# One load per branch, written ahead in the order of use, and the embedding's work beside the last expert, in the mixture-of-experts layer of a two-layer decoder on one Trainium2 core

## The chip, the cores and the metric

The kernel runs on one core of one Trainium2 chip. Its engines are TensorE (PE for the products, PEld for the loads of the stationary operand), VectorE (DVE), ScalarE (ACT), GpSimd (POOL) and SyncE (SP, which issues most transfers). The metric is device microseconds of one execution, lower is better. Three runs of the kernel before took 1607.78 to 1609.05 us, with a median of 1608.46 us.

## The reference, cut to what matters

Two layers over 256 tokens of 1024 channels. Layer 0 has a dense SwiGLU, layer 1 a mixture of 8 experts of which each token takes 2. After the feed-forward part both layers add an embedding that is gated by the residual stream.

```python
def swiglu(x, w1, w3, w2):
    return (jax.nn.silu(x @ w1) * (x @ w3)) @ w2

def moe_swiglu(x, router, w1, w3, w2):
    logits = (x @ router).astype(jnp.float32)
    top_vals, top_idx = lax.top_k(logits, TOP_K)
    ...
    for e in range(N_EXPERTS):
        y = y + comb[..., e:e + 1] * swiglu(x, w1[e], w3[e], w2[e])
...
        x = layer_norm(ALPHA * x + f.astype(x.dtype), ln_g[i, 1], ln_b[i, 1])
        e = (p[i] @ ple_proj[i]) * jax.nn.sigmoid(x @ ple_gate_w[i] + ple_gate_b[i])
        x = layer_norm(ALPHA * x + e.astype(x.dtype), ln_g[i, 2], ln_b[i, 2])
```

Everything is f32. w1 and w3 of an expert are 1024 x 3584, w2 is 3584 x 1024, so one expert reads 42 MB of weights and eight read 336 MB.

## The kernel before, in words

The profile's first 600 us are layer 0 and the mixer of layer 1, which the change does not touch. Then comes `moe`. The router finds each expert's tokens, `gather` (L1393) collects an expert's up to 128 tokens with one-hot products, for two experts at a time (`pair`), and `expert` multiplies them.

**Weights.** An expert has 42 loads of [128, 2048] f32, 1 MB each (`expert_loads`): for each of three chunks of 1024 hidden columns 4 loads of w1 and 4 of w3, for the last chunk of 512 columns 2 and 2, then 14 loads of w2. They are issued by SP at L249 (`load`) into a ring of 18 tiles (`self.ring`): two `rb`, four `st`, `pp`, `ra`, four `hl`, `xl`, two `re`, two `over` and one `raw` of the layer's own pool. A load can start when the products on its tile's previous load are done. The first 8 loads (`EARLY`) are written ahead of the router, every other one just before its use. The order in which each engine's queue holds its instructions is made by the framework's scheduler from its own estimate, so the order of writing is not always the order of issue.

**Branches.** TensorE alone branches on the expert's number of tokens (`either`, L1412): with up to 64 tokens two products run side by side on half the array each ("few"), with more they run one after the other ("many"). One branch holds two loads (`GRP = 2`), that is 21 branches per expert. Work that is to stand between branches (transposes of the hidden tile, the scatter of an expert's result) lies in a list `todo`, which `flush` empties after a branch.

**PSUM.** Six banks go round: a pair for w1, one for w3, one for w2, two for the scatter. `gate` work (Silu on ACT, product on DVE, L1475 and L1476) stands right behind a chunk's products. A pair's unused halves are cleared first (L1432).

**Expert 6.** At `e == OVF` the list is emptied, a branch over the overflow code (more than 128 tokens for one expert) is taken on all engines (L1538, L1539), and the two `over` tiles are free for loads only behind it. Expert 6's first 16 loads are written ahead of it.

**End.** Behind the last expert come its scatter and the second layer norm (`norm`, L524 to L532, `make_xT` L334), `ple_late` (the embedding's input and projection are loaded, split into a high and a low part, L313 and L314, and multiplied, `pp`), then `ple_gate`: the gate's weights are split (`square_parts`, high part L551 on ACT, low part `glo` L553 on POOL and DVE), multiplied for the first and then the second 128 tokens (`pg`, L308 to L310 and L565), and the last layer norm writes the output.

Of the kernel before, what the change touches and what calls it, by code (L numbers as in the profile page):

```python
# [7 lines left out]
F32 = mybir.dt.float32  # L8
F32R = mybir.dt.float32r
# [145 lines left out]
EARLY = 8  # L155
# [3 lines left out]
GRP = 2  # L159
# [21 lines left out]
CHUNKS = ((0, 1024), (1024, 1024), (2048, 1024), (3072, 512))  # L181

# [10 lines left out]
class Trunk:  # L193
# [58 lines left out]
    def room(self, dt, name):  # L252

        pool, tag, n = self.ring[self.nload % len(self.ring)]
        self.nload += 1
        return pool.tile([P, 2048], dt, tag=tag, name=name, bufs=n)

# [846 lines left out]
    def ple_late(self, l):  # L1104

        a = self.a
        n = 2 * S
        self.ring, self.nload = self.turned((self.xp, "pp")), 0
        self.pp = self.xp.tile([P, TT, D], F32, tag="pp", name="pp")
        pT = list(self.parts(self.load(a["pT"][l].rearrange("(k p) t -> p k t", p=P), 2, S), 2, S, self.nc.gpsimd))  # L1110
        w = list(self.parts(self.load(a["ple_proj"][l].rearrange("(k p) f -> p k f", p=P), 2, D), 2, D, self.nc.gpsimd))
        yield
        for tt in range(TT):
            ts = slice(tt * P, (tt + 1) * P)
            for h in range(2):
# [4 lines left out]
                self.nc.scalar.activation(self.pp[:, tt, hs], ps, AF.Copy, scale=0.5)  # L1120
                yield
# [17 lines left out]
    def ple_gate(self, l, raws, low, normed, bias, lnp):  # L1139
# [3 lines left out]
        sp = self.square_parts(range(KT), lambda k: raws[k // 2][:, k % 2], low)  # L1143
        for k in range(KT):

            with self.after(*normed) if k >= GK[l] else ExitStack():
                parts = next(sp)
# [88 lines left out]
    def moe(self, l, mp):  # L1236
# [7 lines left out]
        self.ring.append((mp, "raw", 1))  # L1244
        self.pre = [self.load(*s) for s in self.expert_loads(j, 0)[:EARLY]]
# [92 lines left out]
        for e in range(NE):  # L1338
            if e == OVF:

                self.flush()
                ov = self.over
                main = self.turned(ov[:2])
                self.ring, self.nload = main, 0
                self.pre = [self.load(*s) for s in self.expert_loads(j, e)[: len(main)]]
                self.ring, self.nload = [ov] * ov[2], 0
                pre, self.pre = self.pre, []
                self.overflow(j, mp, Da[:, e // 2 % 2], cint, th, tl, rank, sel, comb, y)
                self.ring, self.pre, self.nload = main + self.ring, pre, len(main)
# [11 lines left out]
            self.expert(mp, self.expert_loads(j, e), n, self.xh[:, :, es], De, [D2[:, tt] for tt in range(TT)], ce, y, ahead, norm if last else None)  # L1361
            if e == NE - 2:

                lnp = self.ln_params(l, 1, mp, "tl")
                more = mp.tile([P, 2, D], F32R, tag="th", name="more")
# [325 lines left out]
```

## Time and profile before

| | us |
|---|---|
| median of 3 runs | 1608.46 |
| the profiled execution | 1610.99 |
| its span from the first to the last instruction | 1608.8 |
| PE busy in the span | 1454.2 (90%) |
| DVE / ACT / POOL busy | 678.0 / 401.3 / 266.0 |
| moved by transfers | 445.28 MB, mean 277 GB/s |

A row of a view of stretches has the stretch in us from the span's start, its length, then for PE, PEld, DVE, ACT and POOL the busy time with the number of instructions, the granted TensorE clock as a share of 2.4 GHz, the busy share of the 16 DMA engines, and GB/s. A row of the timeline has start, duration, engine, line, operation, what it writes and reads, and in brackets the idle time before it and what ended it. A row of the groups has count, busy time, mean ns of one, and the idle time before with what ended it. Ends of products are modelled, so a product's row can overlap the next one's.

### The profile page before, as it was taken

Reading aid. Unit: us, or ns where it says so; the run is one execution under the profiler, and the core shown is the slowest. Engines: PE = TensorE matmul, PEld = TensorE weight load, DVE = VectorE, ACT = ScalarE, POOL = GpSimd, SP = SyncE. Lnnn points to the kernel's source line nnn. Section 1 sums busy time; section 2 is a strip of 40 time slices with the busy share of each in tenths; the row PEclk is TensorE's granted clock in tenths of the full one; section 3 lists DMA queues with packets and bytes.
Section 4 is the critical chain, followed back from the end, with each engine's and each line's share of the span. In section 5 each row is a group of like instructions: output and inputs, shape, how many; then the busy total and the mean of one; then the engine's idle time right before and its main releaser. Section 6 shows DMA issues by size and latency. Waiting matters only on the chain. (4 is left out here: it accounts for less than half of the span.)

```text
span 1608.8 us, 16526 instructions
## 1 busy us (share of the span) xinstructions
PE 1454.2 (90%) x6318; PEld 832.5 (52%) x6319; DVE 678.0 (42%) x1105; ACT 401.3 (25%) x719; POOL 266.0 (17%) x205
## 2 busy tenths in 40 slices
PE   6776999999888699998899999999999998998776
PEld 6544788876675475432344643444644454342234
DVE  8989648646778955222121103121102102122137
ACT  6454555434466431100001001000000000000023
POOL 4855106612124511000000000000000000010012
PEclk9787999999998888999999999999999999999999
DMA  7431365553462049999999999999898878999971
GB/s 250 137 152 40 124 214 187 192 170 131 170 192 111 27 158 401 403 408 405 407 409 402 409 344 389 408 410 400 299 308 272 301 238 281 362 408 409 402 288 53
DMA packets 139625, 445.28 MB, mean 277 GB/s; under 512 B 7408, under 2 KB 19312, under 8 KB 138496
## 3 DMA queue, kind: packets, MB, share of 16 engines
q1 hardware_dynamic: 138496, 437.42, 73.3%
q0 software_dynamic: 1024, 6.38, 1.1%
q8 instruction: 76, 1.25, 0.3%
q14 instruction: 29, 0.24, 0.0%
HBM read 442.72 MB, written 1.05 MB: 276 GB/s over the span
## 5 line engine op out<-in xcount | busy, mean ns | idle before, releaser
L1468 PE MATMUL mgu<-wraw,xe 128*64 128x512 f32 (+3 forms) x2048 | 548.5, 542 | 25.4 <-DMA wraw<-in_moe_w_dram 17.3
L1468 PEld LDWEIGHTS mgu<-wraw,xe 128*64 128x64 f32 (+1 forms) x2048 | 238.3, 157 | 318.4 <-issue 246.9
L1503 PE MATMUL mo<-wraw,ht 128*64 128x512 f32 (+1 forms) x896 | 272.0, 595 | 12.4 <-DMA wraw<-in_moe_w_dram 12.4
L1503 PEld LDWEIGHTS mo<-wraw,ht 128*64 128x64 f32 (+1 forms) x896 | 101.0, 157 | 172.0 <-issue 143.1
L314 DVE TENSOR_TENSOR whl<-wraw,whl 128x1024 fp32r<-128x1024 f32 (+2 forms) x106 | 136.5, 1297 | 81.7 <-ACT whl L313 81.1
L313 ACT ACTIVATE whl<-wraw 128x1024 fp32r<-128x1024 f32 (+3 forms) x109 | 107.5, 994 | 138.3 <-PE fffn_w L310 44.6
L1476 DVE TENSOR_TENSOR hb<-hb,mgu 128x512 f32<-128x512 f32 (+1 forms) x64 | 37.9, 618 | 236.1 <-PE mgu L1468 235.7
L510 POOL DMA_DIRECT2D lnp<-in_lnp_dram x5 | 2.8, 566 | 772.6 <-ACT xe L1397 744.1
L1449 ACT ACTIVATE ht<-hT 128x512 f32<-128x512 f32 (+1 forms) x32 | 17.4, 544 | 393.4 <-PE hT L1444 378.0
L314 DVE TENSOR_TENSOR ot<-mo,ot 128x512 fp32r<-128x512 f32 x16 | 10.6, 688 | 243.1 <-ACT ot L313 243.1
L1432 DVE MEMSET mgu<- 64x512 f32 x128 | 62.1, 485 | 100.2 <-ACT hb L1475 84.1
L1447 DVE COPY ht<-hT 128x512 f32<-128x512 f32 (+1 forms) x32 | 20.0, 625 | 140.7 <-PE hT L1444 136.7
L310 PE MATMUL fffn_w<-whl,xh 128*128 128x512 f32 (+1 forms) x192 | 71.8, 374 | 0.0
L309 PE MATMUL fffn_w<-whl,xl 128*128 128x512 f32 (+1 forms) x192 | 71.7, 373 | 0.0
L308 PE MATMUL fffn_w<-whl,xh 128*128 128x512 f32 (+1 forms) x192 | 71.4, 372 | 0.0
L1475 ACT ACTIVATE hb<-mgu 128x512 f32<-128x512 f32 (+1 forms) x64 | 32.4, 543 | 152.1 <-PE mgu L1468 149.0
L313 ACT ACTIVATE ot<-mo 128x512 fp32r<-128x512 f32 x16 | 9.0, 596 | 239.6 <-PE mo L1503 239.6
L957 DVE SCALAR_TENSOR_TENSOR cy<-upad,pk,cy 128x256 f32<-128x256 f32 x60 | 56.6, 943 | 1.2
L308 PEld LDWEIGHTS fffn_w<-whl,xh 128*128 128x128 f32 x192 | 36.1, 188 | 6.7
L309 PEld LDWEIGHTS fffn_w<-whl,xl 128*128 128x128 f32 x192 | 36.1, 188 | 6.6
L310 PEld LDWEIGHTS fffn_w<-whl,xh 128*128 128x128 f32 x192 | 36.1, 188 | 6.2
L1444 PEld LDWEIGHTS hT<-sqr,hb 128*128 128x128 f32 x224 | 24.8, 140 | 24.7 <-issue 20.4
(371 smaller groups left out, 2147.0 us busy)
## 6 DMA issues: line engine op xcount, KB each, us to landing
wraw<-in_moe_w_dram SPq DMA_DIRECT2D x336, 1024.0 KB, 17.5
wraw<-in_ffn_w_dram SPq DMA_DIRECT2D x33, 1024.0 KB, 5.2
wraw<-in_cmp_w_dram SPq DMA_DIRECT2D x8, 1024.0 KB, 5.6
wraw<-in_w_out_dram SPq DMA_DIRECT2D x8, 1024.0 KB, 7.2
wraw<-in_ple_gate_w_dram SPq DMA_DIRECT2D x8, 1024.0 KB, 5.0
wraw<-in_w_in_dram SPq DMA_DIRECT2D x8, 792.0 KB, 5.9
wraw<-in_w_in_dram SPq DMA_DIRECT2D x8, 768.0 KB, 8.0
lnp<-in_lnp_dram POOLq DMA_DIRECT2D x5, 1024.0 KB, 5.2
```

The source lines that it names most:

```text
L308: mm(dst, xh, wh, start=start, stop=False)
L309: mm(dst, xl, wh, start=False, stop=False)
L310: return mm(dst, xh, wl, start=False, stop=stop)
L313: h = self.hi = self.nc.scalar.activation(dh, src, AF.Copy)
L314: return h, (low or self.nc.vector).tensor_tensor(dl, src, dh.bitcast(F32), op=ALU.subtract)
L957: nc.vector.scalar_tensor_tensor(y0, u(0, k), w(0, k), y0, op0=ALU.mult, op1=ALU.add)
L1432: nc.vector.memset(acc[h][rows[1 - h]], 0.0)
L1444: nc.tensor.transpose(ps[:, i * P : (i + 1) * P], hbs[h][:, i * P : (i + 1) * P], self.ident)
L1468: mm(dst, x, wk, start=k == 0, stop=k == KT - 1)
L1475: nc.scalar.activation(hb[:, :hw], accs[0][h][:, :hw], AF.Silu)
L1476: nc.vector.tensor_mul(hb[:, :hw], hb[:, :hw], accs[1][h][:, :hw])
L1503: mm(dst, x, w[:, i, h * 512 : (h + 1) * 512], start=k == 0, stop=k == NK - 1)
```

## The change

1. The ring gives way to a list of loads (`specs`) and a list of free tiles (`slots`). `feed` writes loads into free tiles, `take` hands the next one to its branch, `give` returns its tile behind the branch and feeds again. So 18 loads are written ahead of the router, and each later one right behind the branch that frees its tile.
2. One load per branch: 42 branches per expert, two loads' work no longer share one.
3. `flush` runs only what was in the list; what these items append waits for the next branch. The gate work, the transposes, the copies out of PSUM, the split of an expert's result, its scatter and its additions each move one branch later than the one ahead. The round of PSUM banks moves on by two after the scatter.
4. The embedding's input, projection and gate weights (0.25 + 1 + 4 MB) stand in the list ahead of the last expert's 14 loads of w2. `ple_early` writes their split and the embedding's products between that expert's last branches, the low parts going into tiles that come free at the end. For the last expert the tiles `pp`, `hl` and `xl` are no longer refilled, so 12 are left, and 8 once the gate's four raw tiles are held.

```diff
@@ -152,11 +152,10 @@
-EARLY = 8
...
-GRP = 2
+LOADS = 42
...
+DOWN = D_FFE // P // 2
@@ -254,6 +255,31 @@
+    def feed(self):
...
+        while self.slots and self.nspec < len(self.specs):
+            pool, tag, n = slot = self.slots.pop(0)
+            if slot == self.over and OVF * LOADS <= self.nspec and self.kept is not None:
+                self.kept.append(slot)
+            elif tag not in ("pp", "hl", "xl") or self.nspec < (NE - 1) * LOADS:
+                src, a, b = self.specs[self.nspec]
+                v = pool.tile([P, 2048], F32, tag=tag, name="wraw", bufs=n)[:, : a * b].rearrange("p (a b) -> p a b", a=a)
+                self.nc.sync.dma_start(v, src)
+                self.fifo.append((v, slot))
+                self.nspec += 1
...
+    def give(self):
+        self.slots += self.used
+        self.used = []
+        self.feed()
@@ -1101,15 +1127,23 @@
-    def ple_late(self, l):
...
+    def ple_early(self, l, mp):
...
+        pT, w = [list(self.parts(self.take(), 2, b)) for b in (S, D)]
+        self.give()
+        raws = [self.take() for _ in range(4)]
+        self.used = []
+        yield
         self.pp = self.xp.tile([P, TT, D], F32, tag="pp", name="pp")
...
+        sp = self.square_parts(range(KT), lambda k: raws[k // 2][:, k % 2], low)
+        for k in range(KT):
+            while k % 2 == 0 and not self.slots:
+                yield
+            self.gate_parts = next(sp)
+            if k % 2:
                 yield
@@ -1241,8 +1291,12 @@
-        self.ring.append((mp, "raw", 1))
-        self.pre = [self.load(*s) for s in self.expert_loads(j, 0)[:EARLY]]
+        self.specs = [s for e in range(NE) for s in self.expert_loads(j, e)]
+        self.specs[-DOWN:-DOWN] = self.ple_specs(l)
+        self.nspec, self.fifo, self.kept, self.used = 0, [], [], []
+        self.slots = self.turned() + [(mp, "raw", 1)] + [(self.st, "hl", HB)] * HB + [(self.cp, "xl", 1)]
+        self.feed()
@@ -1401,8 +1449,10 @@
     def flush(self):
-        while self.todo:
-            self.todo.pop(0)()
+        todo, self.todo = self.todo, []
+        for f in todo:
+            f()
@@ -1455,82 +1520,100 @@
-                for u0 in range(0, KT // ku, GRP):
-                    ws = get()
+                for u in range(KT // ku):
+                    w = get()
...
+            self.todo.append(lambda ci=ci, hw=hw, accs=accs: gate(ci, hw, accs))
         acc = pair("mo")
         NK = D_FFE // P
-        for g in range(0, NK // 2, GRP):
-            ws = get()
+        for g in range(NK // 2):
+            if late:
+                next(late, None)
+            w = get()
...
+        def result():
+            for h in range(2):
+                ot = mp.tile([P, 2, 512], F32R, tag=f"h{h}", name="ot", bufs=1)
+                self.split(ot[:, 0], ot[:, 1], acc[h])
+                ots.append(ot)
+            self.todo.append(scatter)
...
+            def adds():
+                for tt in range(TT):
+                    for h in range(2):
+                        add(tt, h, scs[tt][h])
...
+                self.turn += 2
```

## Rows read from the trace of the kernel before

**Rows 1.** The page: GB/s in 40 equal slices of the span, 40.2 us each

```profile
GB/s 250 137 152 40 124 214 187 192 170 131 170 192 111 27 158 401 403 408 405 407 409 402 409 344 389 408 410 400 299 308 272 301 238 281 362 408 409 402 288 53
```

**Rows 2.** Stretches of experts 1, 2 and 5, and of expert 7 in two parts

```profile
709.00:809.00 100.00, 82.71 (x407) 30.33 (x404) 17.49 (x36) 8.48 (x17) 0.00 (x0) 1.00 1.03 407
809.00:960.00 151.00, 150.58 (x410) 74.54 (x412) 21.19 (x39) 8.19 (x16) 0.00 (x0) 1.00 1.01 394
...
1199.00:1350.00 151.00, 149.94 (x408) 74.06 (x406) 19.73 (x36) 7.88 (x15) 0.00 (x0) 1.00 0.84 277
...
1441.00:1512.00 71.00, 59.69 (x296) 22.66 (x292) 17.62 (x31) 7.28 (x14) 3.44 (x2) 1.00 1.03 405
1512.00:1548.00 36.00, 27.95 (x118) 7.36 (x116) 1.18 (x3) 1.01 (x2) 0.52 (x1) 1.00 1.03 408
```

**Rows 3.** The same view behind the start of expert 6

```profile
1366.00:1370.00 4.00, 4.00 (x22) 1.29 (x18) 0.00 (x0) 0.00 (x0) 0.00 (x0) 1.00 0.91 323
1370.00:1376.00 6.00, 6.00 (x30) 2.01 (x28) 0.00 (x0) 0.00 (x0) 0.00 (x0) 1.00 0.69 272
1376.00:1380.00 4.00, 4.00 (x20) 1.29 (x18) 0.00 (x0) 1.08 (x2) 0.00 (x0) 1.00 0.80 269
```

**Rows 4.** Waits of SP's queue from 1349 to 1385: total, times, longest us

```profile
SPq L249 <- PE mgu L1468: 16.3, 4, 8.2
```

**Rows 5.** Waits of PE from 809 to 1350, and its branches in that stretch (min/median/max)

```profile
PE mgu L1468 <- DVE mgu L1432: 2.1, 2, 1.5
PE DT L1486 <- ACT ht L1449: 1.0, 4, 0.3
PE mgu L1468 <- ACT hb L1475: 0.7, 1, 0.7
...
L1412 PEldq COMPARE_BRANCH  x146: 65/169/340, 811.5 to 1341.7; - x146
```

**Rows 6.** Transfers issued from 1529 to 1560: count, KB each, us to landing

```profile
wraw<-in_ple_gate_w_dram SPq DMA_DIRECT2D x4, 1024.0 KB, 16.6
...
wraw<-in_ple_proj_dram SPq DMA_DIRECT2D x1, 1024.0 KB, 17.2
wraw<-in_pT_dram SPq DMA_DIRECT2D x1, 256.0 KB, 16.9
```

**Rows 7.** Timeline behind the last expert: its last product, then the layer norm

```profile
1546.09 1.94 PE L1503 MATMUL mo<-wraw,ht 128*64 128x512 f32 x8 [0.66 <-DMA wraw<-in_moe_w_dram]
...
1552.88 0.21 DVE L524 BATCH_NORM_AGGREGATE mv<-bst 128x2 f32<-128x12 f32 x1
1553.12 2.79 DVE L531 SCALAR_TENSOR_TENSOR x<-x,mv,lnp 128x512 f32<-128x512 f32 x1
...
1559.38 0.75 DVE L532 SCALAR_TENSOR_TENSOR x<-x,rs,lnp 128x512 f32<-128x512 f32 x1
```

**Rows 8.** Groups from 1546 to 1609: POOL's low parts, ACT's tables, PE's embedding products

```profile
L553 POOL TENSOR_TENSOR glo<-wraw,whi 128x512 fp32r<-128x512 f32 x8 | 11.8, 1512 | 8.9 <-ACT whi L551 8.9
...
L310 PE MATMUL pp<-whl 128*128 128x512 f32 x8 | 4.4, 554 | 3.5 <-POOL whl L314 3.5
...
L526 ACT ACT_TABLE_LOAD x3 | 3.8, 1283 | 0.1
```

**Rows 9.** Timeline of the gate's products: start, 13 without a wait, second half

```profile
1566.19 0.73 PE L565 MATMUL pg<-more,sqr 33*128 33x512 f32 x2
...
1584.12 0.39 PE L308 MATMUL pg<-whi,xh 128*128 128x512 f32 x1
...
1586.91 0.39 PE L310 MATMUL pg<-glo,xh 128*128 128x512 f32 x1
1587.23 0.50 PE L565 MATMUL pg<-more,sqr 33*128 33x512 f32 x1
```

**Rows 10.** Stretches behind the last expert, 4 us each

```profile
1556.00:1560.00 4.00, 2.20 (x6) 1.49 (x5) 3.94 (x3) 0.60 (x1) 2.13 (x1) 0.61 0.17 32
1560.00:1564.00 4.00, 4.00 (x13) 3.20 (x12) 0.13 (x1) 0.89 (x2) 0.00 (x0) 0.54 0.57 232
```

More of the change, by code (lines that the diff above doesn't have):

```diff
@@ L1137, in ple_bias, with ple_gate @@
         return out
-    def ple_gate(self, l, raws, low, normed, bias, lnp):
+    def ple_gate(self, l, raws, low, normed, bias, lnp, parts=None):
         nc = self.nc
         x = self.x
-        sp = self.square_parts(range(KT), lambda k: raws[k // 2][:, k % 2], low)
+        sp = iter(()) if parts else self.square_parts(range(KT), lambda k: raws[k // 2][:, k % 2], low)
         for k in range(KT):
-            with self.after(*normed) if k >= GK[l] else ExitStack():
-                parts = next(sp)
+            with self.after(*normed) if k >= GK[l] and not parts else ExitStack():
+                parts = next(sp, parts)
         for tt in range(TT):
@@ L1339, in moe @@
             if e == OVF:
[L1341 to L1347, printed above, removed]
+                while self.todo:
+                    self.flush()
+                self.ring, self.nload = self.kept, 0
                 self.overflow(j, mp, Da[:, e // 2 % 2], cint, th, tl, rank, sel, comb, y)
-                self.ring, self.pre, self.nload = main + self.ring, pre, len(main)
+                self.slots, self.kept = self.slots + self.kept, None
+                self.feed()
                 pair(e)
@@ L1360, in moe @@
             last = e == NE - 1
-            self.expert(mp, self.expert_loads(j, e), n, self.xh[:, :, es], De, [D2[:, tt] for tt in range(TT)], ce, y, ahead, norm if last else None)
+            late = self.ple_early(l, mp) if last else None
+            self.expert(mp, None, n, self.xh[:, :, es], De, [D2[:, tt] for tt in range(TT)], ce, y, ahead, norm if last else None, late)
             if e == NE - 2:
                 lnp = self.ln_params(l, 1, mp, "tl")
-                more = mp.tile([P, 2, D], F32R, tag="th", name="more")
-                bias = self.ple_bias(l, mp.tile([P, D], F32, tag="h2", name="gb"), more[:, 0])
-        advance(self.ple_late(l))
-        raws = list(self.ple_load(l))
-        low = [t[:, i] for t in [self.room(F32R, "glo").rearrange("p (a d) -> p a d", a=2) for _ in range(4)] for i in range(2)]
+                bias = self.ple_bias(l, mp.tile([P, D], F32, tag="h2", name="gb"), mp.tile([P, D], F32R, tag="th", name="gbr"))
         lnp = self.ln_params(l, 2, mp, "tl")
-        self.ple_gate(l, raws, lambda k: low[k], normed[0], bias, lnp)
+        self.ple_gate(l, None, None, normed[0], bias, lnp, self.gate_parts)
     def expert_loads(self, j, e):
@@ L1415, in either, with expert @@
                 emit(True)
+            self.give()
         self.flush()
-    def expert(self, mp, loads, n, xe, Dm, D2, comb, y, ahead=None, done=None):
+    def expert(self, mp, loads, n, xe, Dm, D2, comb, y, ahead=None, done=None, late=None):
         nc = self.nc
         mm = nc.tensor.matmul
-        loads = iter(loads)
-        get = lambda: [self.pre.pop(0) if (s := next(loads)) and self.pre else self.load(*s) for _ in range(GRP)]
+        loads = iter(loads or ())
+        get = lambda: self.take() if n is not None else self.load(*next(loads))
         rows = (slice(0, SM), slice(P - SM, P))
```

120 lines of the change are left out of this document (70 added, 50 removed).

## Prediction, made before the changed kernel ran

> **What bounds the kernel now.** I read the slices of the page first, to see where transfers run at their limit [rows 1]: from the sixteenth slice on (about 604 us, the experts) most stand at 400 GB/s and more, but those from 1125 to 1407 us stand at 238 to 362. Then stretches, one per expert [rows 2]. Expert 1 (709 to 809) has the array busy 82.71 of 100 us at 407 GB/s: transfers set its pace. Expert 2 (809 to 960) is a "many" expert, busy 150.58 of 151 us, and so is expert 5, at 149.94 of 151 us with 277 GB/s: there the array sets the pace and the tiles are full. Expert 7 has 59.69 of 71 and 27.95 of 36 us at 405 to 408 GB/s: transfers again. A load of 1 MB (1.049 MB) at 408 GB/s takes 2.57 us. Behind the last product of w2, which ends at 1548.0, 60.8 us follow to the span's end at 1608.8 [rows 7].
>
> So a microsecond counts in four places: a load that lands earlier ahead of expert 1; a wait of the array between 809 and 1350; a gap in the transfers behind the start of expert 6, because from there to the last load they are never idle; and what lies between the last load and the end.
>
> **The change, part by part.**
>
> *Loads written ahead.* There are 18 tiles before and after, so no more can be in flight. Expert 1 waits for transfers, and its end moves only if a load starts before the router's tiles come free. The layer's own `raw` tile moves from the fifth place of the round to the thirteenth. If SP's queue keeps that order, one load is later; if the scheduler, which now sees all 18 at once, puts free tiles first, one may be earlier. No row shows that, so the bounds are one load, -2.6 to +2.6 us; I take 0, as both ends are equally near.
>
> *The refill at expert 6.* SP waits four times for products there, 16.3 us in all and 8.2 us once, though a "few" expert frees a tile with every load [rows 4]. From 1366 to 1380 the transfers run at 323, 272 and 269 GB/s [rows 3]. Against 408 that loses 4 x 0.21 + 6 x 0.33 + 4 x 0.34 = 4.2 us. Once each load is written right behind the branch that frees its tile, SP should ask for tiles as they come free. Ends: 0 (the queue's order stays) and 4.2; I take 3.0, nearer to the upper end, because 8.2 of the 16.3 us is one wait.
>
> *Waits of the array, 809 to 1350.* The array waited 2.1 us for the clearing of a pair, 0.7 us for Silu and 1.0 us for the hidden tile's copy [rows 5], 3.8 us in all. The clearing waits are those of w3 of an expert's first chunk, whose banks are w1's own before; the two added turns give it others. The copy's wait falls as the transposes and their copies lie a branch apart. What is late next is the addition of the scattered result, now one branch closer to the pair that reuses its banks, and the gate work, which stands one branch later on ACT and DVE. Ends: 3.8 gained, 3 lost (new waits about as large as the old). I take 2.5, because DVE is busy for only 21.19 of 151 us there [rows 2].
>
> *Twice the branches.* From 809 to 1350 the array's sequencer made 146 branch instructions, 0.169 us at the median [rows 5], and 146 more follow. Costed alone that is 24.7 us. What hides them is the array's own queue: expert 2 has all its branches inside 151 us of which 0.4 are idle [rows 2]. I take 0; without that cover it is 24.7. The Trainium skill gives a price too (Advanced Engine Details and Errata, Control Flow Timing): about 108 ns for a compare-and-branch, by which the exposed sum would be an estimated 15.8 us; the trace's median is higher, and the time by the page would be 1617.5 if none were hidden.
>
> *The embedding ahead of w2.* Its input, projection and gate weights, 0.25 + 1 + 4 MB [rows 6], go in front of the last 14 loads. At 2.57 us per MB that is 13.5 us by which the last product moves, to 1561.5. They fill SP's queue earlier and nothing else queues there; POOL's and ACT's splits wait for landings beside products that wait longer. The embedding's products (three lines of 4.4 us [rows 8]) fit into the 13.5 us in which the array waits for w2, and cost nothing; without that cover they cost about 13.
>
> *What is left behind the last product.* The layer norm's statistics end 5.1 us behind it [rows 7], unchanged. Then an operation of DVE took 2.79 us while POOL split the projection, against 0.75 us for its like at 1559.38 [rows 7]. Without POOL's work I count a table load of 1.28 [rows 8] and 1.4 us of small steps with one 0.75 to the first half, then some 2.2 us of transposes and copies: the gate's products begin 10.0 us behind, now 18.2 (1566.2) [rows 9]. The first 128 tokens took from 1566.2 to 1587.2, 21.0 us. Twelve steps without a wait took 1586.91 - 1584.12 = 2.79 us, 0.233 each [rows 9]; 48 products and the bias then need 11.9 us. But the array is idle ahead of them, as the embedding's products are gone from there. After such a lull the granted clock was 0.61 and 0.54 for 8 us, half of 2.4 GHz for part of it [rows 10]; I take 5 us at half speed, which adds 2.5: 14.4. The second half and the last norm keep their 21.6 us (1587.2 to 1608.8). Sum: 10.0 + 14.4 + 21.6 = 46.0, against 60.8. The gain of 14.8 less 13.5 leaves 1.3 us. Ends: 3.8 without the low clock; and -5.3 if the low parts (11.8 us of POOL [rows 8]) get their tiles too late, so that the first half stays at 21.0.
>
> **Sum.** 0 + 3.0 + 2.5 + 0 + 1.3 = 6.8 us. The profiled execution took 1610.99, 2.5 above the median of 1608.46; on the median it gives 1601.7 us.
>
> **Rivals.** A measurement of this kernel can tell about 0.2%, 3.2 us, from no change: below 1605.2 is faster, above 1611.7 slower.
>
> *The queue keeps its order.* If the scheduler issues as before, writing ahead changes nothing: the refill gives 0 and new waits replace the old. Left is 1.3: 1607.2. For it: the same framework orders the queue; 18 tiles stay 18. Against: each load now stands by the branch that frees its tile. Chance 0.10.
>
> *The split comes too late.* The low parts only get tiles once all loads are written, that is behind the seventh load of w2. If the split then holds the gate's products as now: 6.8 - 6.6 = 0.2 gained, 1608.3. For it: POOL needs 11.8 us and the array waited for it. Against: seven loads of w2 take 18 us. Chance 0.09.
>
> *Branches that show (slower).* In the "many" experts and expert 3 a second branch per two loads runs the array's queue dry. If half shows: 1601.7 + 12.4 = 1614.1. It decides from 10 us on, 40% of the 24.7. For it: single branches take 0.340 us, twice the median [rows 5]. Against: the 0.4 us of idle time in expert 2 [rows 2]. Chance 0.16, with small room for a ring of 8 tiles that runs dry in the last expert.
>
> **How the numbers follow.** The forecast has 0.65, all of it faster. The two cases near no change make 0.19, the slow one 0.16. The best of all ends is 2.6 + 4.2 + 3.8 + 3.8 = 14.4: 1594.1; I go to 1593, for the refill's loss against 408 GB/s leaves out the time until a queue is full again. Upwards the range takes in both cases of no change and ends at 1613, ahead of the slow case.
>
> **What would show it.** Right: from the start of expert 6 to the last load the stretches stand at 400 GB/s and more, with no wait of SP of 8 us; no wait for clearing between 809 and 1350; the embedding's products between the last w1/w3 product and the first of w2; 46 us from the last product of w2 to the end, with no wait of the gate's products for `glo`. Wrong: PE idle at branches in expert 2; transfers below 400 GB/s in expert 7; a tail above 47.3 us, for then moving the 5.25 MB has cost more than it gave (60.8 - 13.5 = 47.3).

## The result, and the profile after

The changed kernel took 1623.56 us (median of 4 runs, 1622.27 to 1623.91) beside 1608.12 us for the kernel before (4 runs, 1606.28 to 1609.05): a ratio of 1.0096, 95% interval 1.0078 to 1.0113. It is slower by 15.4 us, where 6.8 us of gain were forecast. The profiled execution took 1622.27 us, with a span of 1620.4 us.

The page of the changed kernel, GB/s in 40 slices of 40.5 us (before: [rows 1]):

```profile
GB/s 248 154 133 39 132 216 189 185 175 132 190 156 104 27 218 384 404 409 403 409 409 403 346 276 369 409 409 403 324 265 270 340 246 273 343 409 408 402 330 52
```

The three slices from 891 to 1012 us (346, 276, 369) are lower than before (409, 344, 389). Stretches of the changed kernel: expert 1, experts 2 to 5, then 30 us behind the start of expert 6 (columns as ahead of the prediction; before: [rows 2, 3]):

```profile
709.00:809.00 100.00, 81.57 (x409) 32.78 (x406) 21.76 (x40) 8.86 (x17) 0.00 (x0) 0.97 1.03 406
815.00:1363.00 548.00, 540.49 (x1676) 256.12 (x1672) 83.11 (x152) 33.16 (x63) 0.00 (x0) 1.00 0.92 341
...
1366.00:1376.00 10.00, 5.60 (x31) 4.78 (x32) 4.63 (x10) 0.60 (x1) 0.00 (x0) 0.83 0.48 173
1376.00:1386.00 10.00, 8.86 (x45) 4.57 (x43) 1.99 (x5) 1.20 (x2) 0.60 (x1) 1.00 1.03 390
1386.00:1396.00 10.00, 10.00 (x49) 5.97 (x47) 0.00 (x0) 0.72 (x2) 0.00 (x0) 1.00 0.72 252
```

Expert 1 still runs at the transfers' pace. But experts 2 to 5 end at 1363 instead of 1349.5, and behind the start of expert 6 the transfers still fall to 252 GB/s. There SP waits longer in all than before, 21.7 us, though no single wait is as long (from 1363 to 1400; before: [rows 4]):

```profile
SPq L269 <- PE mgu L1532: 21.7, 6, 6.2
```

The waits of the array from 809 to 1350 (before: [rows 5]; total, times, longest):

```profile
PE mgu L1532 <- DMA wraw<-in_moe_w_dram: 8.3, 1, 8.3
PE mgu L1532 <- DVE mgu L1483: 6.1, 5, 1.5
```

Clearing was to vanish and has grown from 2.1 to 6.1 us, and there is one wait of 8.3 us for a load. The timeline shows where it stands:

```profile
798.37 1.94 PE L1566 MATMUL mo<-wraw,ht 128*64 128x512 f32 x8 [0.62 <-DMA wraw<-in_moe_w_dram]
808.61 6.21 PE L1532 MATMUL mgu<-wraw,xe 128*128 128x512 f32 x8 [8.30 <-DMA wraw<-in_moe_w_dram]
814.75 1.94 PE L1566 MATMUL mo<-wraw,ht 128*64 128x512 f32 x8
```

This is the thing to see. `mo` on `128*64` is w2 of expert 1 (up to 64 tokens), `mgu` on `128*128` is w1 of expert 2. The array stops in the middle of expert 1's w2, waits 8.30 us for the first load of expert 2, multiplies that, and goes back to w2 of expert 1, whose loads had landed meanwhile. The branches no longer stand in the order in which they are written. TensorE's own queue in the built program says it outright; loads are numbered in the order of writing, expert e has 42e to 42e + 41, and here is the order of use at the end of expert 1 and the start of expert 2:

```
before    76 77 78 79 80 81 82 83 | 84 85 86 87 88 89 90 91 92 93 94 95
changed   76 77 78 79 80 84 81 85 82 86 83 87 88 92 89 93 90 94 91 95
```

Both mixtures are here: four branches of the next expert's w1 (84 to 87) between the last three of w2 (81 to 83), and four of the second chunk's w1 (92 to 95) between those of the first chunk's w3 (88 to 91). SP issues in the order of writing, so the array waits for load 84 while 81 to 83 land, one every 2.57 us, and lie ready. What the wait costs is their work, three times 1.87 us (814.75 to 816.62), put off into a stretch that the array paces.

The end, on the other hand, went as forecast. Behind the last product of w2 (1574.72 + 1.94 = 1576.7) 43.7 us follow, against 60.8 before. Its steps, in a timeline and in the row of the bias products that begin the second half (answers to [rows 7, 9]):

```profile
1574.72 1.94 PE L1566 MATMUL mo<-wraw,ht 128*64 128x512 f32 x8 [0.65 <-DMA wraw<-in_moe_w_dram]
...
1584.73 0.92 PE L334 MATMUL pg<-whi,xh 128*128 128x512 f32 x2 [0.69 <-ACT xh L339]
```

```profile
L591 PE MATMUL pg<-gbr,sqr x3: 381/387/503, 1598.9 to 1608.4; 33*128 33x256 f32 x2, 33*128 33x512 f32 x1
```

The gate's products begin 8.1 us behind it, the first 128 tokens take 14.2 us (1584.7 to 1598.9), the rest 21.5. And the embedding's products did stand in the wait for w2, as two rows of the timeline show (the first of its products, then w2's first after only 3.27 us of wait):

```profile
1529.86 0.50 PE L334 MATMUL pp<-whl 128*128 128x512 f32 x1 [0.20 <-ACT whl L339]
...
1541.49 10.08 PE L1566 MATMUL mo<-wraw,ht 128*64 128x512 f32 x32 [3.27 <-DMA wraw<-in_moe_w_dram]
```

### The profile page after: what moved, and what is told of

The parts are those of the page before. It is cut to its first block, busy times and chain, and to the rows that moved or that the text cites. A ratio compares the mean times of both kernels' runs of the same rounds, so it can differ in the third digit from the quotient of the medians.

```text
span 1620.4 us, 16733 instructions
## 1 busy us (share of the span) xinstructions
PE 1460.6 (90%) x6318; PEld 833.7 (51%) x6319; DVE 676.6 (42%) x1108; ACT 401.5 (25%) x719; POOL 260.1 (16%) x202
## 5 line engine op out<-in xcount | busy, mean ns | idle before, releaser
L1532 PE MATMUL mgu<-wraw,xe 128*64 128x512 f32 (+3 forms) x2048 | 558.3, 549 | 39.0 <-DMA wraw<-in_moe_w_dram 26.0
L1566 PE MATMUL mo<-wraw,ht 128*64 128x512 f32 (+1 forms) x896 | 279.1, 606 | 11.3 <-DMA wraw<-in_moe_w_dram 11.3
L340 DVE TENSOR_TENSOR whl<-wraw,whl 128x1024 fp32r<-128x1024 f32 (+3 forms) x109 | 137.5, 1271 | 84.0 <-ACT whl L339 83.3
L579 POOL TENSOR_TENSOR glo<-wraw,whi 128x512 fp32r<-128x512 f32 x16 | 26.1, 1661 | 148.0 <-PE mo L1566 84.4
```

The lines of the kernel that those rows point to most:

```text
L340: return h, (low or self.nc.vector).tensor_tensor(dl, src, dh.bitcast(F32), op=ALU.subtract)
L579: (nc.gpsimd if n in POOLW else nc.vector).tensor_tensor(lo[:, c : c + 512], src[:, c : c + 512], hi[:, c : c + 512].bitcast(F32), op=ALU. ...
L1532: mm(dst, x, w[:, i, hs], start=k == 0, stop=k == KT - 1)
L1566: mm(dst, x, w[:, i, h * 512 : (h + 1) * 512], start=k == 0, stop=k == NK - 1)
```

## The experiments

All runs are compared with the kernel before, which took 1607.63 to 1608.91 us (medians) beside them.

### 1. The changed kernel with its branches in written order

```diff
-            with self.tc.If(n > SM) as many:
-                emit(False)
-            with many.Else():
-                emit(True)
+            with self.tc.issue_after(self.branch) if self.branch else ExitStack():
+                with self.tc.If(n > SM) as many:
+                    emit(False)
+                with many.Else():
+                    emit(True)
+            self.branch = self.nc.cur_bb.bb.instructions[-1]
```

> The changed kernel with one constraint more: TensorE's branches keep the order in which they are written (each is queued behind the one before). Theory 1: in the changed kernel four branches of the next expert's w1 stand ahead of the last three of w2; at the end of expert 1 the array waited 8.30 us for a load that landed at 808.56 us while three finished loads of w2 lay behind it, about 5.6 us of work, which then had to be done in a stretch where the array sets the pace. In written order the products of expert 2 start at about 809 us with nothing left over, and the whole is about 5.3 us faster than the changed kernel: 1618.3 us. Rival: that stretch is bound by transfers anyway, so the order of the array's work changes nothing: 1623.6 us (within 1).

Measured: 1597.76 us (1596.58 to 1601.71), 0.9938 of before (0.9918 to 0.9958). That is 25.8 us less than the changed kernel, five times what was expected: written order was right, and its price far too low. Stretches of this kernel: experts 2 to 5, then the start of expert 6, and a hole in expert 7:

```profile
806.00:1339.50 533.50, 532.77 (x1661) 257.80 (x1661) 83.14 (x153) 33.01 (x62) 0.00 (x0) 1.00 0.96 356
1350.00:1360.00 10.00, 9.96 (x57) 4.78 (x57) 2.67 (x6) 1.80 (x3) 0.60 (x1) 1.00 1.01 392
1360.00:1370.00 10.00, 10.00 (x50) 3.21 (x46) 3.22 (x6) 1.08 (x2) 0.00 (x0) 1.00 1.01 405
...
1495.00:1500.00 5.00, 0.00 (x0) 0.00 (x0) 0.86 (x2) 1.88 (x3) 0.00 (x0) 0.65 0.58 180
```

In experts 2 to 5 the array is idle for 0.7 us (533.50 - 532.77), and behind the start of expert 6 the transfers are at 392 and 405 GB/s at once: both of the forecast's gains show. A clearing wait is left nowhere in that stretch.

To compare single profiles, count from the first product of expert 0. What lies ahead of it the change does not touch, and yet it starts between 615.4 and 623.4 us in the 16 profiles. Here it is in three timelines: the kernel before, the changed kernel, and this one:

```profile
622.48 20.91 PE L1468 MATMUL mgu<-wraw,xe 128*64 128x512 f32 x96
620.03 1.94 PE L1532 MATMUL mgu<-wraw,xe 128*64 128x512 f32 x8
620.14 1.94 PE L1536 MATMUL mgu<-wraw,xe 128*64 128x512 f32 x8
```

The last two start alike. Expert 5 ends 23.7 us earlier than in the changed kernel (1339.6 against 1363.3). The rows place about 18 of them. One load (2.6 us) was lost early in expert 0, where SP waited for a tile that a mixed order held: the first product of expert 2 starts at 806.0 instead of 808.6. The stretch from 637 to 642 of the changed kernel stands at 252 GB/s, the same one in written order at 409:

```profile
637.00:642.00 5.00, 5.00 (x26) 1.59 (x22) 1.66 (x3) 1.09 (x2) 0.00 (x0) 1.00 0.82 252
```

```profile
637.00:642.00 5.00, 5.00 (x30) 2.03 (x28) 2.67 (x5) 0.60 (x1) 0.00 (x0) 1.00 1.02 409
```

Three loads of w2 were carried into a stretch that the array paces. The groups of the array by shape show 136 products of w2 on half the array in the changed kernel from 815 to 1363, and 112 in written order from 806 to 1339.5; the 24 more make 6.5 us (31.1 - 24.6), or 5.6 by their starts in the timeline above:

```profile
L1566 PE MATMUL mo<-wraw,ht 128*64 128x512 f32 x136 | 31.1, 598 | 0.0
```

```profile
L1570 PE MATMUL mo<-wraw,ht 128*64 128x512 f32 x112 | 24.6, 594 | 0.0
```

The clearing waits are 6.1 us. And behind the wait of 8.30 us the array was slow; stretches of the changed kernel in the wait and behind it:

```profile
804.00:808.60 4.60, 0.00 (x0) 0.00 (x0) 0.00 (x0) 0.00 (x0) 0.00 (x0) 0.50 1.03 410
808.60:814.70 6.10, 6.09 (x8) 2.35 (x8) 0.00 (x0) 0.00 (x0) 0.00 (x0) 0.58 1.03 409
814.70:820.80 6.10, 6.10 (x21) 2.19 (x22) 0.00 (x0) 0.00 (x0) 0.00 (x0) 1.00 1.03 410
```

The granted clock is 0.50 of 2.4 GHz, that is 1.2 GHz, in the last 4.60 us of the wait and 0.58 for the 6.1 us behind it. The eight products took 6.1 us where eight at full clock take some 3.6 (six of the same kind took 2.74 us at 828.58, below): 2.5 us. That is 2.6 + 6.5 + 6.1 + 2.5 = 17.7 us; the other 6 to 7 us I can't place by single rows. The array is idle for 7.5 us of the 548.00 in the changed kernel and for 0.7 us in written order, so most of them are busy time, products that took longer; why, no run shows. Behind expert 5 the two profiles differ by only 0.6 us (257.1 and 256.5 to the span's end): what the quicker refill gave was lost in the hole of expert 7 and in an end of 45.2 instead of 43.7 us.

### 2. The changed kernel without the deferred additions

```diff
-            def adds():
-                for tt in range(TT):
-                    for h in range(2):
-                        add(tt, h, scs[tt][h])
-
-                self.turn += 2
...
+                    with self.after(*normed):
+                        add(tt, h, sc[h])
```

> The changed kernel with the additions of a scattered result back beside its scatter, and without the two turns of the PSUM round behind them. Theory 2: the array's waits for clearing (6.1 us from 809 to 1363, against 2.1 us in the kernel before) come from these two edits: the pair of w3 takes the banks of the scatter, and its clearing stands behind the additions on DVE. Without them the clearing waits fall to about 2 us in that stretch: 1623.6 - 4.0 = 1619.6 us. Rival: w3 then takes w1's own banks and waits for Silu instead, so the sum of the waits stays at about 6 us: 1623.6 us (within 1).

Measured: 1629.69 us (1623.04 to 1629.91), 1.0118 of before (1.0092 to 1.0143): worse in three of four runs, while the fourth is as fast as the changed kernel. Both theory and rival were wrong. The waits for clearing from 809 to 1369 rose:

```profile
PE mgu L1532 <- DVE mgu L1483: 10.3, 5, 2.8
```

So in the scheduler's order the two edits don't cause these waits, they soften them. The timeline of the changed kernel behind expert 1 shows the cause of one of them:

```profile
828.58 2.74 PE L1532 MATMUL mgu<-wraw,xe 128*128 128x512 f32 x6
...
832.05 0.75 DVE L1612 SCALAR_TENSOR_TENSOR x<-sc,comb,x 128x512 f32<-128x512 f32 x1 [2.36 <-PE sc L1593]
...
832.98 0.48 DVE L1483 MEMSET mgu<- 64x512 f32 x1 [0.18 <-DVE x L1612]
...
833.37 1.99 DVE L1612 SCALAR_TENSOR_TENSOR x<-sc,comb,x 128x512 f32<-128x512 f32 x3
...
835.53 0.48 DVE L1483 MEMSET mgu<- 64x512 f32 x1 [0.17 <-DVE x L1612]
836.07 2.41 PE L1532 MATMUL mgu<-wraw,xe 128*128 128x512 f32 x5 [1.42 <-DVE mgu L1483]
```

By the time the scatter (`sc`) runs, four branches of the next w1 are over, so w3 comes right behind it. Its clearing stands on DVE behind three additions (1.99 us), and the array waits 1.42 us. In written order only two branches of w1 lie ahead of the scatter.

### 3. The changed kernel with the embedding's work back at the end

The list of loads loses the six of the embedding, `ple_early` is not called, and `ple_late` and `ple_load` of the kernel before stand behind the last expert:

```diff
-        self.specs[-DOWN:-DOWN] = self.ple_specs(l)
...
-        self.ple_gate(l, None, None, normed[0], bias, lnp, self.gate_parts)
+        advance(self.ple_late(l))
+        raws = list(self.ple_load(l))
...
+        self.ple_gate(l, raws, lambda k: low[k], normed[0], bias, lnp)
```

> The changed kernel with the embedding's loads, products and the gate's split back behind the last expert, and with all 18 tiles in use to the end. Theory 4: the tail alone pays what was forecast and a little more: in the changed kernel the last load came 13.4 us later for it and the tail fell by about 17 us, so without it the time is about 3.7 us longer: 1627.3 us. Rival: the eight tiles left in the last expert and the low parts cost as much as the tail gives: 1623.6 us or less.

Measured: 1619.13 us (1617.06 to 1621.49), 1.0063 of before (1.0045 to 1.0082): 4.4 us less than the changed kernel. The move costs. The last product of w2 ended at 1563.7 (13.0 earlier), and 55.0 us follow, not 60.8: the same code at the end is 5.8 us shorter here than in the kernel before.

### 4. The kernel before with one load per branch

```diff
-GRP = 2
+GRP = 1
...
-            if g == GRP and ahead:
+            if g == 2 and ahead:
```

> The kernel before with one load per branch and nothing else. Theory 3 and 1 together: the scheduler puts the branches of the next expert ahead of the last of w2 here too (about 5.3 us lost at the end of expert 1), and 84 more branches in the four experts that the array paces cost about 0.05 us each, 4.5 us: 1608.1 + 9.8 = 1617.9 us. Rival: single branches are hidden, and the loss of the changed kernel comes from its new list of loads and its work put off by a branch: 1608 to 1610 us.

Measured: 1631.24 us (1629.84 to 1632.29), 1.0138 of before (1.0121 to 1.0155). One constant makes the kernel before 22.8 us slower. Its queue has the same mixture (80 84 81 85 82 86 83 87), and the same two waits from 809 to 1371:

```profile
PE mgu L1468 <- DVE mgu L1432: 10.3, 5, 2.8
PE mgu L1468 <- DMA wraw<-in_moe_w_dram: 8.4, 1, 8.4
```

The list of loads and the deferred work are out of it.

### 5. Written order, with the embedding's work back at the end

The edits of experiments 1 and 3 together.

> The changed kernel with its branches in written order (1597.76 us in the first experiment) and the embedding's work back behind the last expert. Theory: moving the embedding ahead of w2 costs more than it gives. In the ordered kernel the last product ended at 1550.9 us with 45.2 us behind it; the 5.25 MB ahead of w2 take 13.4 us of it and a wait of 11.0 us in the last expert left the transfers idle for about 2.9 us. With the work back the last product should end near 1534.6 us; the tail of the first run with the work back was 55.0 us, so the span is about 1590 us and the time 1591 us. Rival: the tail is that of the kernel before, 60.8 us, and the move is worth nothing either way: 1597 us. The forecast's own reading (the move gains 1.3 us): 1599 us.

Measured: 1594.38 us (1594.32 to 1595.96), 0.9915 of before (0.9898 to 0.9931): 3.4 us less than with the move. It lies between theory and rival, because the end is 59.3 us long (1533.3 to 1592.6). A timeline of this kernel shows 8.13 us of it:

```profile
1538.94 2.00 ACT L340 ACTIVATE whl<-wraw 128x1024 fp32r<-128x1024 f32 x2 [6.35 <-DMA wraw<-in_ple_proj_dram]
...
1540.85 1.06 ACT L340 ACTIVATE ot<-mo 128x512 fp32r<-128x512 f32 x2
...
1541.48 0.80 PE L1617 MATMUL sc<-ot,DT 128*128 128x512 f32 x1 [8.13 <-ACT ot L340]
```

The projection's split waits on ACT for its load, and behind it stands the copy of the last expert's result, which the scatter needs.

### 6. The kernel before with one load per branch, in written order

The edits of experiments 1 and 4 together.

> The kernel before with one load per branch, and its branches in written order. Theory: single branches cost nothing by themselves; what cost 22.8 us in the run with one load per branch was the order into which the scheduler put them. In written order the time is that of the kernel before or a little less: 1605 to 1609 us. Rival: half or more of the loss is the branches' own time on the array's queue (84 more in the four experts that the array paces): 1613 us or more.

Measured: 1600.56 us (1598.78 to 1602.71), 0.9949 of before (0.9932 to 0.9967). Better than the theory: in written order smaller branches cost nothing, and something is gained, 8.2 us in all (experiment 13 splits them). The clearing wait is the old one:

```profile
PE mgu L1472 <- DVE mgu L1436: 2.1, 2, 1.5
```

### 7. Written order, without the deferred additions and the two turns

The edits of experiments 1 and 2 together.

> The changed kernel in written order, with the additions of a scattered result back beside its scatter and without the two turns of the PSUM round. Theory: the two edits did take the clearing waits away, once the branches stand in order (in the ordered kernel the array waited for no clearing between 806 and 1340 us); without them four to five waits of 1 to 1.5 us come back in that stretch: about 1603 us. Rival: written order alone removed the waits, and the edits do nothing: 1597.8 us (within 1).

Measured: 1602.45 us (1600.75 to 1605.3), 0.9966 of before (0.9954 to 0.9979): 4.7 us more than in experiment 1, the theory's time. From 809 to 1344 the old waits are back, three and not the four to five of the theory; from the first product of expert 2 to the end of expert 5 it is 537.5 us, where experiment 1 had 533.5:

```profile
PE mgu L1536 <- DVE mgu L1487: 2.1, 2, 1.5
PE mgu L1536 <- ACT hb L1496: 0.7, 1, 0.7
```

### 8. Written order, with the split queued behind the last gate work

In experiment 1 the array waited 11.0 us in expert 7. A timeline of that kernel:

```profile
1496.92 0.69 DVE L341 TENSOR_TENSOR whl<-wraw,whl 128x512 fp32r<-128x512 f32 x1 [24.41 <-ACT whl L340]
...
1503.03 0.48 DVE L1487 MEMSET mgu<- 64x512 f32 x1 [0.17 <-issue]
1503.11 1.51 PE L1536 MATMUL mgu<-wraw,xe 128*64 128x256 f32 x4 [11.00 <-DVE mgu L1487]
```

DVE stood for 24.41 us at the split of an input that hadn't landed, with the clearing of a pair of the last chunk behind it. The edit:

```diff
-        pT, w = [list(self.parts(self.take(), 2, b)) for b in (S, D)]
-        self.give()
+        two = [self.take() for _ in range(2)]
+        held = self.used[-2:]
         raws = [self.take() for _ in range(4)]
         self.used = []
         yield
+        with self.after(*self.gated):
+            pT, w = [list(self.parts(t, 2, b)) for t, b in zip(two, (S, D))]
+        self.slots += held
+        self.feed()
+        yield
```

> The changed kernel in written order, with the split of the embedding's input and projection one branch later and queued behind the last gate work of the expert on ACT and DVE. Theory: in the ordered kernel the array waited 11.0 us in the last expert (1492.11 to 1503.11) for a clearing that stood on DVE behind this split, which itself waited for its load; the transfers then fell to 178 GB/s for 5 us, a loss of about 2.9 us. Queued behind the gate work the wait goes, and the time is about 1595 us. Rival: that stretch is bound by transfers, the wait only takes the place of waits for loads, and the time stays at 1597.8 us (within 1).

Measured: 1598.29 us (1594.92 to 1599.06), 0.9929 of before (0.9911 to 0.9946): no difference in the medians. The wait is gone and the transfers from 1495 to 1500 are at 389 GB/s; but the array then waits 14.7 us for the first load of w2. The medians fit the rival. The profile fits the theory better: it started expert 0 at 623.4 us instead of 620.1, and from the end of expert 5 to the span's end it takes 254.3 us against 256.6 in experiment 1, so that 2.3 of the theory's 2.9 us show. One pair of profiles doesn't settle it.

### 9. The changed kernel with two loads per branch

Each branch takes two loads (`ws = [get(), get()]`), the rest is as changed, and no order is forced.

> The changed kernel with two loads per branch again, and no constraint on the order. Theory: the loss of the change comes from one load per branch alone, because only then does the scheduler put branches of the next expert ahead of the last of w2; with two loads per branch its own order is the written one, and everything else in the change is worth what was forecast: between the ordered kernel's 1597.8 us and 8 us more (what the finer branches gave in written order): about 1602 us. Rival: the work put off by a branch loses by itself as soon as the scheduler is free to order: 1615 us or more.

Measured: 1606.57 us (1604.41 to 1610.7), 0.9993 of before (0.9983 to 1.0002): no change, and 4.6 us more than the theory's 1602. So with experiment 4, one load per branch alone makes the loss in the scheduler's order; but without it the rest of the change is worth little. The refill at expert 6 is about that of the kernel before [rows 3]; two stretches:

```profile
1366.00:1376.00 10.00, 10.00 (x50) 3.46 (x48) 0.60 (x2) 0.60 (x1) 0.00 (x0) 1.00 0.78 295
1376.00:1386.00 10.00, 10.00 (x52) 3.61 (x48) 2.74 (x5) 1.34 (x3) 0.00 (x0) 1.00 0.84 317
```

The order of use says why. It is the written one in experts 1 to 5 and 7, but not in experts 0 and 6, and there it is the same in the kernel before (expert 6; 252 to 255 and 260 to 263 are w1, 256 to 259 w3):

```
before, two loads (9)   252 253 256 257 260 261 254 255 258 259 262 263
changed                 252 256 260 253 257 261 254 258 262 255 259 263
written order           252 253 254 255 256 257 258 259 260 261 262 263
```

### 10 and 11. Only the embedding's input and projection ahead of w2

On top of experiment 8:

```diff
-        self.specs[-DOWN:-DOWN] = self.ple_specs(l)
+        ps = self.ple_specs(l)
+        self.specs[-DOWN:-DOWN] = ps[:2]
+        self.specs += ps[2:]
...
-            with self.after(*normed) if k >= GK[l] and not parts else ExitStack():
+            with self.after(*(normed if k >= GK[l] else self.result if l else ())):
```

Experiment 11 has 4 instead of 2 in `GK`, the number of high parts that stand ahead of the layer norm.

> The changed kernel in written order, with only the embedding's input and projection (1.25 MB) ahead of w2, and the gate's four weights behind it in the list; the split of the input and projection stands behind the last gate work, and the split of the gate's weights behind the copy of the last expert's result. Theory: 1.25 MB cost 3.2 us and take the embedding's products and the wait of the result's copy (8.1 us in the run with the work back and in order) off the end; the gate's weights land while the layer norm runs. Last product near 1533.3 + 3.2 = 1536.5 us, with about 50 us behind it: 1588 us. Rival: the gate's products then wait for the low parts as in the kernel before, so the end takes 55 us or more: 1593 us or more, no better than with all of it behind (1594.4).

> As the run before this one, with four instead of two of the eight high parts of the gate's weights ahead of the layer norm on ACT. Theory: POOL's and DVE's low parts are what the gate's first products wait for; starting two more of them some 5 us earlier shortens the end by 1 to 3 us: about 1586 us. Rival: the two more copies stand ahead of the norm's table load on ACT and wait for their load there, so the norm is later by as much as the low parts are earlier: within 1 us of the run before this one.

Measured: 1588.44 us (1586.28 to 1590.94), 0.9887 of before (0.9870 to 0.9903), the best of all; and 1594.32 us (1592.97 to 1594.64), 0.9916 (0.9900 to 0.9933). The first hit its theory: the last product at 1536, 48.5 us behind it, and the result's copy right behind the product. The first norm of this kernel still keeps the array waiting:

```profile
1535.90 1.09 ACT L340 ACTIVATE ot<-mo 128x512 fp32r<-128x512 f32 x2 [22.57 <-PE mo L1562]
...
1544.16 1.11 PE L361 MATMUL xtr<-sqr,x 128*128 128x128 f32 x4 [4.85 <-DVE x L559]
```

With four high parts that wait is 10.29 us, for the low parts on DVE stand ahead of the norm: neither theory nor rival had that as the larger effect.

### 12. Order kept at the ends of the experts alone

`issue_after` with the last branch of the expert before, for all branches of an expert, so that only w1 and w3 within an expert may mix.

```diff
+            with self.tc.issue_after(self.fence) if self.fence else ExitStack():
...
+            self.fence = None if e in (0, OVF) else self.branch
```

> The changed kernel with a weaker constraint: no branch of an expert is queued ahead of the last w2 branch of the expert before it, but within an expert the scheduler may order as it likes (it puts branches of w3 between those of w1). Theory: most of the 25.8 us that written order gave comes from the ends of the experts, where w2 of one and w1 of the next were mixed (the array's 8.30 us wait, the clearing behind the scatter, the change between the two kinds of branch); what is left for the mixing within experts is one load of 2.6 us at the start and a slower refill: about 1603 us. Rival: mixing w1 and w3 within an expert holds tiles just as long, and half or more of the loss stays: 1611 us or more.

Measured: 1606.59 us (1602.98 to 1608.31), 0.9994 of before (0.9980 to 1.0007). So 17.0 of the 25.8 us come from the ends of the experts, and 8.8 from the mixing of w1 and w3 within them. In the profiles, counted from expert 0's first product, the latter is 7.6 us: 2.5 ahead of expert 2, 3.6 in experts 2 to 5 (537.1 against 533.5) and 1.5 behind them. The theory had the larger part right and the smaller one too small. There is no clearing wait between 809 and 1340; but expert 6 is still used in a mixed order (252 256 260 253 257), and behind its start the transfers fall:

```profile
1370.00:1380.00 10.00, 10.00 (x48) 5.79 (x45) 1.36 (x3) 1.15 (x2) 0.00 (x0) 1.00 0.62 199
```

### 13 and 14. Written order with two loads per branch

The edit of experiment 1 on the kernel before (13) and on the kernel of experiment 9 (14).

> The kernel before, two loads per branch, with its branches in written order and nothing else. In its own queue the loads of experts 0 and 6 are used out of order (of expert 6: 252 253 256 257 260 261 254 255 258 259 262), those of the other experts in order. Theory A: the 8.2 us that the run with one load per branch in written order gained over the kernel before come from the smaller branches, which free a tile with every load: 1608 us here (within 1.5). Theory B: they come from written order at experts 0 and 6, where the refill was slow because tiles came free in another order than SP asks for them: 1600 to 1603 us here, with the transfers at 390 GB/s or more soon behind the start of expert 6.

> The changed kernel with two loads per branch, in written order. Without the constraint it took 1606.57 us, in written order with one load per branch 1597.76 us. Theory A (smaller branches): written order changes little with two loads, 1605 to 1607 us. Theory B (order at experts 0 and 6): most of the 8.8 us between those two runs is order, 1598 to 1601 us.

Measured: 1605.14 us (1600.46 to 1608.03), 0.9979 of before (0.9966 to 0.9992); and 1599.73 us (1599.48 to 1600.12), 0.9936 (0.9919 to 0.9953). The first lies between the theories. Of the 8.2 us of experiment 6, written order makes 3.4 to 3.8 (by the ratio and by the medians; interval 1.3 to 5.5), the smaller branches the other half. In the second nearly all is order: 6.8 us from experiment 9 to 14, and 2.0 from there to experiment 1 (9.2 and -0.3 by the ratios). Counted from expert 0's first product the profiles agree: 986.3 us before, 983.3 (13) and 978.2 (6); 983.8 (9), 977.1 (14) and 976.0 (1). But theory A, that smaller branches gain because they free a tile with every load, isn't borne out. From 13 to 6 experts 2 to 5 gain 2.0 us (540.5 and 538.5), the time from there to the last product is 5.2 us longer (195.3 and 200.5), and what follows is 8.5 us shorter (61.1 and 52.6): most of the other half lies at the end of the kernel. The refill of the kernel before in written order, where [rows 3] had 272 and 269 GB/s:

```profile
1360.00:1370.00 10.00, 10.00 (x48) 3.30 (x46) 1.11 (x3) 1.08 (x2) 0.00 (x0) 1.00 0.97 373
1370.00:1380.00 10.00, 10.00 (x48) 3.16 (x44) 2.11 (x4) 0.00 (x0) 0.00 (x0) 1.00 1.03 402
```

## Why the prediction was wrong

**The step that failed** is "Twice the branches". It asked what a branch costs on the array's sequencer and what hides it, and that answer was right: in written order the array is idle for 0.7 of 533.5 us. It did not ask in what order twice as many, smaller branches would be queued. My own description of the kernel said that the scheduler orders each queue by its own estimate, and a rival dealt with SP's order; neither looked at TensorE's. Experiments 4, 6, 1 and 9 close this: one load per branch costs the kernel before 22.8 us in the scheduler's order, and in written order it gains 4 to 5; the changed kernel gains 25.8 us from written order alone, and 17.0 from two loads per branch. What I could have seen beforehand is the other half of it: the array takes its products strictly in order, so whatever stands ahead of a landed load holds it. The 8.30 us in which three loads land unused are the row for that, and the Trainium skill (PSUM — Partial Sum Buffer, Engine vs sequencer instructions) has products start and complete in program order. The price for a compare-and-branch, which the prediction had weighed, played no part.

**Branches that show**, the rival on the slower side, had the sign, and a size between half of its 24.7 us (1614.1) and all of them (1626.4), but not the mechanism: the array's waits are for a load and for clearing, not for its queue.

**The queue keeps its order**, a rival near no change, came true in two of its steps, for the refill gave nothing and new waits replaced the old; its time did not. **The split comes too late** did not happen: behind the last product no product of the gate waits for a low part.

**Loads written ahead** (0, from -2.6 to 2.6). In written order the first product of expert 2 starts at 806.0 instead of 808.9, but 2.3 of these 2.9 us lie ahead of expert 0, in what the change does not touch. From expert 0's first product to expert 2's it is 186.43 us before, 185.85 in written order and 188.58 in the changed kernel. So the term measured 0.6 us, near the 0 that was taken, and the changed kernel lost one load to the mixed order of expert 0.

**The refill at expert 6** (3.0). The forecast put SP's waits down to where a load is written. They came from the order of use in expert 6, mixed already in the kernel before; with the loads written ahead and that mixture the transfers stayed slow (experiments 9 and 12). In written order the refill was quick without any list of loads: in experiment 13 the time from the end of expert 5 to the last product falls from 198.6 to 195.3 us. These 3.3 us are the size that was forecast, from another cause.

**Waits of the array** (2.5). In written order it is 533.5 us from the first product of expert 2 to the end of expert 5, against 540.5 before: 7.0 us, near three times the forecast. The deferred additions and the two turns make 4.0 of them (experiments 1 and 7; 4.7 by the medians). In the scheduler's order the clearing waits tripled: "what is late next" named the additions and the gate work, but not that w3 would come right behind the scatter.

**The embedding ahead of w2 and the end** (+1.3). The steps hold almost to the row: 8.1 + 14.2 + 21.5 = 43.7 us (rounded) against 10.0 + 14.4 + 21.6 = 46.0. The move gains nothing all the same: it costs 3.4 to 4.4 us by the medians, and 0.7 and 2.5 in the profiles counted from expert 0's first product. The comparison was mis-sized: 60.8 us is not what the old end takes beside the new experts. Put back, it took 55.0 and 59.3 us. In the kernel before, SP issues one of the gate's weights ahead of the projection:

```profile
1532.24 2.31 SPq L249 DMA_DIRECT2D wraw<-in_ple_gate_w_dram  x1
1534.60 0.46 SPq L249 DMA_DIRECT2D wraw<-in_ple_proj_dram  x1
```

Where it does so the old end takes 59.0 to 61.1 us (before, experiments 4 and 13); where the projection goes first, 55.0 and 52.6 (experiments 3 and 6); in experiment 5 the projection was issued only behind the last product. The forecast took the 60.8 us as fixed. That this order makes the difference was not tested by itself. In written order the move also held up expert 7: counted from the end of expert 5, the last product came 16.7 us later (211.4 against 194.7) instead of 13.5. There one of the prediction's signs of being wrong came: in expert 7 the transfers stand at 386 GB/s (1444 to 1548), where the kernel before had 406 (1441.5 to 1546). The best kernel has 1.25 MB ahead of w2 and 4 MB behind (experiment 10), but it also has the splits in a better order, and what of its gain is the smaller move was not separated.

With the branches in written order the changed kernel takes 1597.76 us: inside the range, 3.9 us under the forecast. Counted from expert 0's first product, its profile is 10.3 us shorter than that of the kernel before (976.0 against 986.3): 0.6 ahead of expert 2, 7.0 in experts 2 to 5 and 2.7 behind them, where 0, 2.5 and 3.0 + 1.3 were forecast. That the sum came so near is in part luck, as errors of the terms cancel in part.

## What to carry to other kernels

Where a scheduler orders the queues, making pieces smaller or more independent is a change of order: compare the order of use on each engine with the order in which the transfers are issued before costing anything else. If an engine takes its work in order and the transfers come in order, force the two to be the same. Here one constraint was worth 25.8 us on the changed kernel and 3.4 to 3.8 on the one before, and turned the smaller pieces from a loss of 22.8 us into a small gain. Compare single profiles from the point where the change begins: here the untouched part ahead of it varied by up to 8 us. A step whose input is still on its way must not be queued ahead of a short one that somebody waits for: waits of 8.1 and 11.0 us came from that on ACT and DVE, though taking the second out changed the medians by nothing.

## What the runs showed of the hardware that was not expected

A wait of 8.30 us of the array cost more than the work put off by it: the granted clock was 0.50 of 2.4 GHz (1.2 GHz) towards its end and 0.58 in the 6.1 us behind it, where eight products took some 2.5 us more than at full clock. Twice the branches cost the array nothing that shows: with 42 branches per expert it was busy for 532.8 of 533.5 us.
